# A two-block transformer kernel on one core: who empties PSUM and splits the weights, when the second layer's conditioning is streamed, and how the planner sets priorities

## The chip, the cores and the metric

The kernel runs on one core of a Trainium2 chip. It uses TensorE (PE) for matrix products, VectorE (DVE) and ScalarE (ACT) for all elementwise work, GpSimd (POOL) for a little preparation, and the queue of SyncE (SP) for nearly all DMA. The metric is the device time of one execution in microseconds (us). Before the change it is 1009.37 us, the median of three runs (1007.86 to 1009.71).

## The reference

256 tokens of width 1024 pass through a first block of two layers and a second block of two layers. Cut to what matters here:

```python
cond = silu(c)
for i in range(2):                                   # first block
    sh1, sc1, g1, sh2, sc2, g2 = split(cond @ ada_w[i] + ada_b[i], 6)
    h = rms_norm(x, norm_mix[i]) * (1 + sc1) + sh1
    y = chunked_relpos_attention(h, ...) if i == 0 else chunked_spatial_gating(h, ...)
    x = x + g1 * y
    h = rms_norm(x, norm_ffn[i]) * (1 + sc2) + sh2
    x = x + g2 * (square(relu(h @ ffn_w1[i])) @ ffn_w2[i])
for l in range(2):                                   # second block
    proj = rms_norm(x, pre_norm[l]) @ w_in[l]
    ya = differential_attention(...) * silu(ag)      # 4 heads
    yb = grouped_query_attention(...) * silu(bg)     # 8 heads
    x = x + rms_norm(concat(ya, yb) @ w_out[l], post_norm[l])
```

The attention of the first block has 16 heads of width 64 and a relative-position bias; each token sees its own chunk of 64 and all earlier ones. The gating layer (gMLP) applies gelu to 6144 columns, normalises half of them, mixes positions in windows of 128 and multiplies. All data is fp32.

## The kernel before, in words

**Products.** Tokens lie in two halves of 128, t=0 and t=1. Each fp32 operand is split into a high part (rounded to fp32r) and a low part (the rest), and a product is three fp32r matmuls, high by high, high by low and low by high (`mm3`, L782 to L784). Transposes (`tr`, L810) and the attention's own small matmuls (L770) are fp32.

**Weights.** All weights come as items of 128 x 1024 in the order of `stream_items`, in loads of two items (1 MB, L842) into four `raw` slots. A weight item is split on chip by `item`: a cast to the high part (ACT, L881, or DVE, L882) and a subtraction to the low part (DVE, L885). A slot is free again when its items have been used. Conditioning weights (`ada_w`) run through the same slots, but DVE multiplies them with the condition vector, either as a dot product per 128 rows of a transposed block (`adc`, L748 plus an accumulator read) or as a scaled add into a row (`adg`, L740), after which `fin_gate` spreads the row. (l, m) names the m-th of the six vectors of layer l; `BY_ROWS` lists those that use the second way.

**Stages.** `run` calls attention, FFN0, gMLP, FFN1 and the second block's layers 0 and 1. The attention first projects the eight row blocks k into six PSUM banks (`w("aqk", k)`, `w("avq", k)`), then computes scores, softmax (ACT's Exp, L695, with DVE's L748 for bias and maximum), values and the output projection (weights `ao`). `out_proj` projects t=0 and t=1 into two banks each (c=0, 1). `resid` multiplies by the gate and adds to x (L721), `sumsq` sums squares (L931 on ACT, L933 on DVE), `norm_scale` computes 1/rms with Ln and Exp and scales (L968, L970), and `transpose_split` transposes, applies the conditioning (L1015, L1021) and splits (L988 on ACT, L990 on DVE) into the operands of the next stage.

**Who runs what, and when.** Every operation goes into a planner (`Sched`). An operation may have alternatives on two engines. `round` plays a model timeline: on each engine it takes, among the operations that can start about now, the one with the smallest priority number; the sequence that comes out is each engine's fixed program order. `schedule` repeats this four times: after each round every operation gets a due time, worked backwards from its users, and the next round takes the due times as priorities. The sequence of the best round by the model's clock is kept. ACT's function tables (exp, gelu, silu) are loaded where the order needs another one (L1642).

Of the kernel before, what the change touches and what calls it, by code (L numbers as in the profile page):

```python
# [47 lines left out]
BY_ROWS = ((0, 2), (0, 5), (1, 2), (1, 5), (0, 3))  # L48
# [10 lines left out]
def stream_items():  # L59
    s = []  # L60
    for k in range(KT):
        s += [("adc", 0, 1, k), ("adc", 0, 0, k), ("aqk", k), ("avq", k)]
    for x, y in ((ada_items(0, (2, 4)), [("a2", j, 1, q) for j in (1, 2) for q in range(4)]),
                 (ada_items(0, (3,)), [("ao", k) for k in range(KT)])):
        n = len(y)
        for i, it in enumerate(y):
            s.append(it)
            s += x[len(x) * i // n:len(x) * (i + 1) // n]
    s += pair_stream(NFF, ("w1", 0), ("w2", 0), LAGF, ada_items(0, (5,)) + ada_items(1, (0, 1, 2)))
    e = ada_items(1, (3, 4, 5))  # L70
    for g in range(6):
        for q in range(4):
            s.append(("bv", g, q))
            if len(e) > 12:
                s.append(e.pop(0))
    s += pair_stream(NCB, ("bu",), ("bo",), LAG, e)
    s += pair_stream(NFF, ("w1", 1), ("w2", 1), LAGF)
    for l in range(2):
        s += [("xs", l, BQ, q) for q in range(4)]
        s += [("kv", l, q) for q in range(2)]  # L80
        s += [("ws", l, AQ + 128 * i) for i in range(4)]
        s += [("ws", l, AK + 128 * i) for i in range(4)]
        for c in (AV, AG, BG):
            s += [("xs", l, c, q) for q in range(4)]
        s += [("so", l, k) for k in range(KT)]
    return s
# [244 lines left out]
class Sched:  # L331
# [6 lines left out]
    EXTRA = {"DVE": 0.6}  # L338

# [60 lines left out]
    def schedule(self, spaces, slots, rounds=4):  # L400
# [4 lines left out]
        for i in range(rounds):  # L405
# [6 lines left out]
            if best is None or self.clock < best[0]:  # L412
                best = self.clock, [(o, alt, tab, [b.off for b in o.bufs]) for o, alt, tab in out], \
                    {b: b.off for b in self.fixed}, [(o, o.eng, o.start, o.fin) for o in self.ops]
            due = {}
            for o in sorted(self.ops, key=lambda o: o.start, reverse=True):
                t = o.start if o.eng == "PE" else self.clock
                for u in o.users:
                    if o in u.deps:
                        t = min(t, due[u] - latency(o, u.eng) - (o.fin - o.start))  # L420
                due[o] = t
            for o in self.ops:
                o.pri = due[o] - (self.RUSH if o.crit else 0.0)
        self.clock = best[0]
        for o, o.eng, o.start, o.fin in best[3]:
            pass
        for b in self.fixed:
            b.off = best[2][b]
        return best[1]
# [226 lines left out]
class Prog:  # L656
# [188 lines left out]
    def item(self):  # L845
# [30 lines left out]
        else:  # L876
# [6 lines left out]
            self.prev_split = S.op(alts[:1] if i < POS["w1", 0, 0] else alts, [src], [hi], after=after, pri=pri,  # L883
# [222 lines left out]
    def setup(self):  # L1106
# [15 lines left out]
        self.hooks[1] = [lambda pri: load(self.x[1].v(), io["xin"][:, 1, :], 1.46, pri)]  # L1122
# [12 lines left out]
    def attention(self):  # L1135
# [54 lines left out]
        for j, n in ((0, 0), (1, 0), (2, 0), (0, 1)):  # L1190
            for t in range(2):
                self.copy(qkv[j][n][t].v(), acc[t, j + 3 * n].v(), 512, psum=True)

        def second(j):
# [6 lines left out]
            for t in range(2):  # L1201
                self.copy(qkv[j][1][t].v(), ps[t].v(), 512, psum=True)
# [19 lines left out]
        for i in range(4):  # L1222
            self.act(nb[i].v(), nb[i].v(), D, scale=-1.0, dve=True)
# [4 lines left out]
        for h in range(16):  # L1228
# [4 lines left out]
            if h % 2 == 0:  # L1233
# [4 lines left out]
                self.act(qT.v(), ps.v()[:, 0:256], 256, scale=gqk.v(), psum=True, dve=True)  # L1238
                kk = kd[blk % 2]
                for i in range(2):  # L1240
                    self.copy(kk.v(i)[i * 64:(i + 1) * 64, i * 256:(i + 1) * 256], ps.v()[i * 64:(i + 1) * 64, 256:512], 256,
                              psum=True)
# [16 lines left out]
            self.copy(pT.v(), ps.v()[:, 0:384], 384, psum=True)  # L1259
# [29 lines left out]
    def ffn(self, l):  # L1289
# [5 lines left out]
        gate = self.mod(l, 5) if l == 1 else None  # L1295
# [368 lines left out]
```

## Time and profile before

| | |
|---|---|
| median of three runs | 1009.37 us |
| the profiled execution, its own time | 1009.61 us |
| its span | 1007.8 us |
| PE busy | 976.2 us (97%) |
| DVE busy | 776.7 us (77%) |
| ACT busy | 568.0 us (56%) |
| mean granted TensorE clock | 0.992 |
| chain that ended last | PE 79%, DVE 9%, ACT 5%, DMA 4% |

The span is what the profiler saw from the first to the last instruction; the time of a run includes a little around it. Busy times of engines overlap, so they don't add up. "Idle before" is time in which an engine had nothing it could do, with the instruction that released it. All tiles of a kind lie in one large buffer (`arena` for fp32, `arena_r` for split operands, `raw` for loaded weights, `banks` for PSUM), so the rows tell an operation by its line and shape.

### The profile page before, as it was taken

The page shows a single profiled execution, that of the slowest core. Times are in us where ns is not written, and L with a number is a line of the kernel's source. Part 1 is how long each engine was busy: PE and PEld are TensorE (multiplying, and loading weights), DVE is VectorE, ACT ScalarE, POOL GpSimd, SP SyncE. Part 2 cuts the span into 40 slices and gives each one's busy share as a digit, 9 for nine tenths or more (in the row PEclk, how much of TensorE's full clock was granted, in tenths as well). Part 3 has the DMA queues.
Part 4 walks back from the last instruction along what each step waited for, and adds up shares of the span by engine and source line. Part 5 has one row for each costly group of instructions (what it writes and reads, how often), then busy time and mean ns, then how long its engine had stood idle before and what let it go on. Part 6 is the DMA issues. An engine that isn't in the chain of part 4 may idle for free.

```text
span 1007.8 us, 14849 instructions
## 1 busy us (share of the span) xinstructions
PE 976.2 (97%) x5716; PEld 851.7 (85%) x5716; DVE 776.7 (77%) x1308; ACT 568.0 (56%) x1052; POOL 24.7 (2%) x60
## 2 busy tenths in 40 slices
PE   6999988999999999999999999999999999899997
PEld 5768776899999888899999899999989888799886
DVE  6899989988877986977767855645697786877982
ACT  6578736544445655644455744445455676655781
POOL 1000000010000000000000000030000000000000
PEclk9999998999999999999999999999999999899999
DMA  8987585898775595766463555565545333443401
GB/s 321 359 316 263 210 334 183 359 364 324 290 281 203 207 383 204 292 228 232 170 242 133 177 197 172 207 193 203 179 161 188 113 121 119 160 168 128 166 1 42
DMA packets 32121, 216.50 MB, mean 215 GB/s; under 512 B 3825, under 2 KB 4081, under 8 KB 7217
## 3 DMA queue, kind: packets, MB, share of 16 engines
q1 hardware_dynamic: 30816, 211.98, 56.9%
q0 software_dynamic: 1232, 3.56, 1.4%
q8 instruction: 45, 0.74, 0.3%
q14 instruction: 28, 0.22, 0.1%
HBM read 214.48 MB, written 1.05 MB: 214 GB/s over the span
## 4 chain that ended last, share of the span: by engine, by line
PE 79%; DVE 9%; ACT 5%; DMA 4%; issue 2%; SPq 0%; DVEq 0%; ACTq 0%
PE banks L782 24%; PE banks L783 24%; PE banks L784 24%; PE banks L770 4%; DMA raw<-in_wall 4%; DVE arena_r L885 3%; PE banks L810 3%; DVE arena L721 2%; ACT arena_r L881 1%; ACT arena L695 1%; DVE arena L740 1%; DVE arena L748 1%; DVE arena_r L990 1%; DMA arena<-in_xin 1%; ACT arena L710 1%
## 5 line engine op out<-in xcount | busy, mean ns | idle before, releaser
L782 PE MATMUL banks<-arena_r 128*128 128x256 f32 (+1 forms) x1632 | 563.9, 346 | 7.7 <-ACT arena_r L988 5.2
L783 PE MATMUL banks<-arena_r 128*128 128x256 f32 (+1 forms) x1632 | 554.0, 339 | 1.5 <-DVE arena_r L885 1.4
L784 PE MATMUL banks<-arena_r 128*128 128x256 f32 (+1 forms) x1632 | 553.4, 339 | 1.6 <-DVE arena_r L990 1.6
L885 DVE TENSOR_TENSOR arena_r<-raw,arena_r 128x1024 fp32r<-128x1024 f32 x300 | 359.7, 1221 | 41.8 <-ACT arena_r L881 40.4
L782 PEld LDWEIGHTS banks<-arena_r 128*128 128x128 f32 x1632 | 310.9, 191 | 43.3 <-ACT arena_r L988 8.9
L784 PEld LDWEIGHTS banks<-arena_r 128*128 128x128 f32 x1632 | 310.5, 190 | 38.3 <-DVE arena_r L990 4.7
L783 PEld LDWEIGHTS banks<-arena_r 128*128 128x128 f32 x1632 | 311.2, 191 | 35.3 <-DVE arena_r L885 4.6
L881 ACT CAST arena_r<-raw 128x1024 fp32r<-128x1024 f32 x265 | 270.5, 1044 | 85.9 <-DMA raw<-in_wall 43.4
L695 ACT ACTIVATE arena<-banks 128x256 f32<-128x256 f32 (+1 forms) x104 | 45.0, 434 | 147.2 <-PE banks L784 145.1
L988 ACT ACTIVATE arena_r<-arena 128x256 fp32r<-128x256 f32 (+1 forms) x120 | 55.8, 475 | 78.5 <-DVE arena L740 49.6
L740 DVE SCALAR_TENSOR_TENSOR arena<-banks,arena 128x256 f32<-128x256 f32 (+1 forms) x84 | 38.1, 453 | 60.7 <-ACT arena L695 42.8
L748 DVE CUSTOM_DVE_ANT_0 arena<-raw,arena 128x1024 f32<-128x1024 f32 x56 | 71.7, 1281 | 14.5 <-DMA raw<-in_wall 13.1
L695 ACT ACTIVATE arena<-arena 128x256 f32<-128x256 f32 (+8 forms) x159 | 65.1, 416 | 23.9 <-DVE arena L740 9.1
L990 DVE SCALAR_TENSOR_TENSOR arena_r<-arena,arena_r 128x256 fp32r<-128x256 f32 (+1 forms) x120 | 58.3, 494 | 24.6 <-ACT arena_r L988 23.1
L770 PE MATMUL banks<-arena 128*128 128x64 f32 (+4 forms) x448 | 70.3, 292 | 4.5 <-DMA arena<-in_ident 3.6
L770 PEld LDWEIGHTS banks<-arena 128*128 128x128 f32 x448 | 60.6, 196 | 10.1 <-ACT arena L695 3.6
L810 PE MATMUL banks<-arena 128*128 128x128 f32 x356 | 55.7, 281 | 10.1 <-DVE arena L731 4.3
L710 ACT COPY arena<-banks 128x512 f32<-128x512 f32 (+4 forms) x100 | 47.7, 488 | 31.2 <-PE banks L784 13.7
L810 PEld LDWEIGHTS banks<-arena 128*128 128x128 f32 x356 | 44.0, 147 | 21.5 <-DVE arena L731 4.6
L721 DVE TENSOR_TENSOR arena<-arena 128x512 f32<-128x512 f32 (+6 forms) x128 | 51.4, 433 | 7.6 <-ACT arena L695 3.2
L740 DVE SCALAR_TENSOR_TENSOR arena<-raw,arena 128x1024 f32<-128x1024 f32 x40 | 51.3, 1282 | 3.8 <-DMA raw<-in_wall 3.6
L721 DVE TENSOR_TENSOR arena<-banks,arena 128x512 f32<-128x512 f32 (+1 forms) x48 | 30.0, 641 | 15.3 <-PE banks L784 6.8
(45 smaller groups left out, 330.5 us busy)
## 6 DMA issues: line engine op xcount, KB each, us to landing
raw<-in_wall SPq DMA_DIRECT2D x194, 1024.0 KB, 4.9
raw<-in_wall SPq DMA_DIRECT2D x8, 512.0 KB, 9.1
arena<-in_nbias SPq DMA_DIRECT2D x4, 512.0 KB, 6.5
arena<-in_rows POOLq DMA_DIRECT2D x3, 512.0 KB, 6.0
arena<-in_xin SPq DMA_DIRECT2D x2, 512.0 KB, 5.9
out_dram<-arena SPq DMA_DIRECT2D x4, 256.0 KB, 2.4
arena<-in_dbias POOLq DMA_DIRECT2D x2, 384.0 KB, 3.6
arena<-in_wsT POOLq DMA_DIRECT2D x1, 512.0 KB, 5.9
```

What stands on the lines that cost most here:

```text
L695: nc.scalar.activation(out=res(out), in_=res(in_), func=func, scale=res(scale), **kw, **({"accum_out": res(accum)} if accum is not None el ...
L721: alt = ("DVE", 0.068 + n / 960.0, lambda: nc.vector.tensor_tensor(out=res(out), in0=res(a), in1=res(b), op=op))
L740: return self.S.op(("DVE", dur, lambda: nc.vector.scalar_tensor_tensor(out=res(out), in0=res(a), scalar=res(s), in1=res(b), op0=op0, op1=o ...
L748: return self.S.op(("DVE", dur, lambda: nc.vector.tensor_tensor_reduce(out=res(junk if out is None else out), in0=res(a), in1=res(b), scal ...
L770: o = self.S.op(("PE", max(n, 96) * 0.00167, lambda: nc.tensor.matmul(res(out), lhsT=res(l), rhs=res(r), start=start, stop=stop)), rd, [ou ...
L782: nc.tensor.matmul(o, lhsT=lh, rhs=rh, start=start, stop=False)
L783: nc.tensor.matmul(o, lhsT=lh, rhs=rl, start=False, stop=False)
L784: nc.tensor.matmul(o, lhsT=ll, rhs=rh, start=False, stop=stop)
L810: nc.tensor.transpose(res(o), res(i), res(ident))
L881: alts = [("ACT", 0.093 + D / 1200.0, lambda: nc.scalar.copy(out=res(hi), in_=res(src))), ("DVE", 0.068 + D / 1920.0, lambda: nc.vector.te ...
L885: dve = ("DVE", 0.068 + D / 960.0, lambda: nc.vector.tensor_tensor(out=res(lo), in0=res(src), in1=res(hi.f32()), op=ALU.subtract))
L990: self.S.op(("DVE", 0.068 + n / 960.0, lambda: nc.vector.scalar_tensor_tensor(out=res(lo), in0=res(src), scalar=scale, in1=res(hi.f32()), ...
```

## The change

Six edits:

1. In the attention, the copies and scalings that empty PSUM, and the scaling of the bias, have only ACT as an alternative (`both=False`, no `dve=True`).
2. The high-part cast of a weight has only ACT as an alternative, in the whole kernel.
3. `(0, 3)` leaves `BY_ROWS`, so it becomes eight dot products and needs no `fin_gate` matmuls.
4. Layer 1's conditioning moves back in the stream: (1, 2) from FFN0 to gMLP, (1, 5) from gMLP to FFN1.
5. x's second half is loaded right after the first, no longer behind the first weight loads.
6. Due times are worked backwards from a PE timeline from which the model's gaps are taken out (`packed`), instead of from the model's own start times. The best round's priorities are played once more. `shift` is added, but `SHIFTS` is empty.

```diff
-BY_ROWS = ((0, 2), (0, 5), (1, 2), (1, 5), (0, 3))
+BY_ROWS = ((0, 2), (0, 5), (1, 2), (1, 5))
...
-    s += pair_stream(NFF, ("w1", 0), ("w2", 0), LAGF, ada_items(0, (5,)) + ada_items(1, (0, 1, 2)))
-    e = ada_items(1, (3, 4, 5))
+    s += pair_stream(NFF, ("w1", 0), ("w2", 0), LAGF, ada_items(0, (5,)) + ada_items(1, (0, 1)))
+    e = ada_items(1, (2, 3, 4))
...
-    s += pair_stream(NFF, ("w1", 1), ("w2", 1), LAGF)
+    s += pair_stream(NFF, ("w1", 1), ("w2", 1), LAGF, ada_items(1, (5,)))
...
             if best is None or self.clock < best[0]:
-                best = self.clock, [(o, alt, tab, [b.off for b in o.bufs]) for o, alt, tab in out], \
...
-            due = {}
+                best = self.clock, [o.pri for o in self.ops]
+
+            due, packed, gaps, last = {}, {}, 0.0, 0.0
+            for o in sorted((o for o in self.ops if o.eng == "PE"), key=lambda o: o.start):
+                gaps += max(o.start - last, 0.0)
+                packed[o], last = o.start - gaps, o.fin
             for o in sorted(self.ops, key=lambda o: o.start, reverse=True):
-                t = o.start if o.eng == "PE" else self.clock
+                t = packed[o] if o.eng == "PE" else last - gaps
...
-            self.prev_split = S.op(alts[:1] if i < POS["w1", 0, 0] else alts, [src], [hi], after=after, pri=pri,
+            self.prev_split = S.op(alts[:1], [src], [hi], after=after, pri=pri,
...
-        self.hooks[1] = [lambda pri: load(self.x[1].v(), io["xin"][:, 1, :], 1.46, pri)]
+        load(self.x[1].v(), io["xin"][:, 1, :], 1.46, -2000)
...
-                self.copy(qkv[j][n][t].v(), acc[t, j + 3 * n].v(), 512, psum=True)
+                self.copy(qkv[j][n][t].v(), acc[t, j + 3 * n].v(), 512, psum=True, both=False)
...
-            self.act(nb[i].v(), nb[i].v(), D, scale=-1.0, dve=True)
+            self.act(nb[i].v(), nb[i].v(), D, scale=-1.0)
...
-                self.act(qT.v(), ps.v()[:, 0:256], 256, scale=gqk.v(), psum=True, dve=True)
+                self.act(qT.v(), ps.v()[:, 0:256], 256, scale=gqk.v(), psum=True)
...
-        gate = self.mod(l, 5) if l == 1 else None
```

Since the planner sets the order, most of what the program does differently is not in the diff. Line numbers of the changed kernel are 14 to 16 higher: L770, L782 to L784 and L810 are L786, L798 to L800 and L826; L881, L885 and L721 are L897, L901 and L737.

VectorE at the end of the output projection, before: the last items of (0, 3) and of `ao` (L740, L885), then the residual and sum of squares of t=0 (L721, L933).

```order
L740 SCALAR_TENSOR_TENSOR arena<-raw,arena 128x1024
L885 TENSOR_TENSOR arena_r<-raw,arena_r 128x1024
L740 SCALAR_TENSOR_TENSOR arena<-raw,arena 128x1024
L885 TENSOR_TENSOR arena_r<-raw,arena_r 128x1024
L882 CAST arena_r<-raw 128x1024
L721 TENSOR_TENSOR arena<-banks,arena 128x512 x2
L721 TENSOR_TENSOR arena<-arena 128x512 x2
L933 ISA arena<-arena 128x512
L933 ISA arena 128x1
L731 TENSOR_SCALAR arena<-arena 128x1
L721 TENSOR_TENSOR arena<-banks,arena 128x512 x2
L968 TENSOR_SCALAR arena<-arena 128x512
```

The same place after:

```order
L901 TENSOR_TENSOR arena_r<-raw,arena_r 128x1024
L764 ISA arena<-raw,arena 128x1024
L764 ISA arena 128x1
L1006 SCALAR_TENSOR_TENSOR arena_r<-banks,arena_r 128x512
L901 TENSOR_TENSOR arena_r<-raw,arena_r 128x1024
L756 SCALAR_TENSOR_TENSOR arena<-arena 128x1
L737 TENSOR_TENSOR arena<-banks,arena 128x512
L737 TENSOR_TENSOR arena<-arena 128x512
L949 ISA arena<-arena 128x512
L949 ISA arena 128x1
L737 TENSOR_TENSOR arena<-banks,arena 128x512
L737 TENSOR_TENSOR arena<-arena 128x512
```

The eight scaled adds have become dot products (L764) that stand between the splits; the last of them comes ahead of the last split (L901). No cast stands between that split and the residual, and the residual's steps follow c by c.

TensorE at the handover from `ao` to FFN0, before: the end of the output projection, the gate's matmuls (L770), the transposes of t=0's normalised rows, and the first product of FFN0.

```order
L783 MATMUL banks<-arena_r 128x512
L784 MATMUL banks<-arena_r 128x512
L770 MATMUL banks<-arena 128x1 x8
L810 MATMUL banks<-arena 128x128 x8
L782 MATMUL banks<-arena_r 128x512
```

And after:

```order
L799 MATMUL banks<-arena_r 128x512
L800 MATMUL banks<-arena_r 128x512
L826 MATMUL banks<-arena 128x128 x8
L798 MATMUL banks<-arena_r 128x512
L799 MATMUL banks<-arena_r 128x512
```

The gate's matmuls are gone. What the products are is told by the planner's names for them, which stand in no row. Before, the products of t=0 and t=1 alternate to the end of `ao` (two of t=1 behind t=0's last), and what follows the transposes is FFN0. After, t=0's products come earlier; the six products ahead of these transposes are t=1's for k = 2 to 4, the six behind them are its for k = 5 to 7, and FFN0 begins behind those.

ScalarE in gMLP, where the gelu of the first column blocks, Ln and Exp of the two halves' norms and the next gelu need other tables, before:

```order
L695 ACTIVATE arena<-banks 128x256
L881 CAST arena_r<-raw 128x1024
L1642 ACT_TABLE_LOAD
L695 ACTIVATE arena<-arena 128x1 x2
L881 CAST arena_r<-raw 128x1024 x2
L1642 ACT_TABLE_LOAD
L695 ACTIVATE arena<-banks 128x256 x2
```

And after:

```order
L711 ACTIVATE arena<-banks 128x256
L1657 ACT_TABLE_LOAD
L711 ACTIVATE arena<-arena 128x1 x4
L897 CAST arena_r<-raw 128x1024
L1657 ACT_TABLE_LOAD
L711 ACTIVATE arena<-banks 128x256 x2
```

Before, Ln and Exp of one half (x2) stand between two loads, with two casts behind them, and the other half's stand ahead of the preceding load of gelu; after, both halves' (x4) stand between one pair of loads with one cast.

## Rows read from the trace of the kernel before

**Rows 1.** The page, its first part: busy us, share, instructions.
```profile
PE 976.2 (97%) x5716; PEld 851.7 (85%) x5716; DVE 776.7 (77%) x1308; ACT 568.0 (56%) x1052; POOL 24.7 (2%) x60
```

**Rows 2.** Windows, a steady stage: us, busy of each engine, clock, DMA share, GB/s.
```profile
200.00:400.00 200.00, 200.00 (x1141) 175.84 (x1141) 165.43 (x239) 100.89 (x161) 3.05 (x5) 1.00 0.75 286
```

**Rows 3.** Timeline of PE, 147 to 166: start, us, engine, line, tiles, idle before.
```profile
147.51 1.84 PE L770 MATMUL banks<-arena 128*128 128x1 f32 x16
150.63 1.09 PE L810 MATMUL banks<-arena 128*128 128x128 f32 x8 [1.28 <-ACT arena L970]
153.55 0.79 PE L782 MATMUL banks<-arena_r 128*128 128x512 f32 x1 [1.82 <-ACT arena_r L988]
154.14 0.63 PE L783 MATMUL banks<-arena_r 128*128 128x512 f32 x1
154.57 0.63 PE L784 MATMUL banks<-arena_r 128*128 128x512 f32 x1
...
160.15 0.48 PE L782 MATMUL banks<-arena_r 128*128 128x512 f32 x1
160.47 0.40 PE L783 MATMUL banks<-arena_r 128*128 128x512 f32 x1
160.70 0.39 PE L784 MATMUL banks<-arena_r 128*128 128x512 f32 x1
...
165.75 0.51 PE L784 MATMUL banks<-arena_r 128*128 128x512 f32 x1 [0.59 <-DVE arena_r L990]
```

**Rows 4.** Windows of the attention.
```profile
64.00:100.00 36.00, 34.76 (x193) 27.93 (x193) 35.06 (x87) 31.70 (x82) 2.07 (x4) 1.00 0.69 250
100.00:130.00 30.00, 29.27 (x165) 22.62 (x164) 29.02 (x76) 20.25 (x58) 1.44 (x2) 1.00 0.55 201
...
140.00:147.00 7.00, 5.77 (x24) 4.22 (x24) 6.54 (x8) 2.77 (x3) 0.00 (x0) 1.00 1.01 408
```

**Rows 5.** Timeline of DVE, end of the output projection.
```profile
143.39 1.22 DVE L885 TENSOR_TENSOR arena_r<-raw,arena_r 128x1024 fp32r<-128x1024 f32 x1
...
145.67 1.37 DVE L721 TENSOR_TENSOR arena<-banks,arena 128x512 f32<-128x512 f32 x2 [0.38 <-PE banks L784]
```

**Rows 6.** Groups by line and shape, DVE in 58 to 147: busy, mean ns, idle.
```profile
L713 DVE COPY arena<-banks 128x512 f32<-128x512 f32 x3 | 2.1, 691 | 1.3 <-PE banks L784 1.3
L701 DVE TENSOR_SCALAR arena<-arena 128x1024 f32<-128x1024 f32 x2 | 1.4, 690 | 0.0
...
L701 DVE TENSOR_SCALAR arena<-banks,arena 128x256 f32<-128x256 f32 x3 | 1.3, 476 | 0.0
```

**Rows 7.** Timelines of DVE and ACT, start.
```profile
15.74 1.28 DVE L748 CUSTOM_DVE_ANT_0 arena<-raw,arena 128x1024 f32<-128x1024 f32 x1
...
26.48 1.05 ACT L881 CAST arena_r<-raw 128x1024 fp32r<-128x1024 f32 x1 [5.61 <-DMA raw<-in_wall]
```

**Rows 8.** Timelines of ACT and PE, gMLP.
```profile
414.87 1.28 ACT L1642 ACT_TABLE_LOAD   x1
...
419.10 1.28 ACT L1642 ACT_TABLE_LOAD   x1
...
420.83 0.39 PE L782 MATMUL banks<-arena_r 128*128 128x256 f32 x1 [1.34 <-ACT arena L695]
```

**Rows 9.** Timeline of PE, second block, layer 0 to 1.
```profile
870.60 1.09 PE L810 MATMUL banks<-arena 128*128 128x128 f32 x8 [1.60 <-DVE arena L968]
873.43 0.79 PE L782 MATMUL banks<-arena_r 128*128 128x512 f32 x1 [1.74 <-ACT arena_r L988]
```

**Rows 10.** Casts of DVE and the window, 780 to 975.
```profile
L882 DVE CAST arena_r<-raw 128x1024 fp32r<-128x1024 f32 x13 | 8.8, 685 | 2.1 <-PE banks L784 2.1
...
780.00:975.00 195.00, 191.34 (x1124) 166.39 (x1123) 154.88 (x334) 131.11 (x297) 2.65 (x5) 0.98 0.36 128
```

**Rows 11.** Waits of the load queue (SP), 60 to 147: us, times, longest.
```profile
SPq L842 <- DVE arena L748: 35.0, 7, 11.0
```

**Rows 12.** The page, its fifth part: the casts of ACT.
```profile
L881 ACT CAST arena_r<-raw 128x1024 fp32r<-128x1024 f32 x265 | 270.5, 1044 | 85.9 <-DMA raw<-in_wall 43.4
```

More of the change, by code (lines that the diff above doesn't have):

```diff
@@ L338 @@
     EXTRA = {"DVE": 0.6}
+    SHIFTS = ()
     def __init__(self):
@@ L412, in schedule @@
             if best is None or self.clock < best[0]:
-                best = self.clock, [(o, alt, tab, [b.off for b in o.bufs]) for o, alt, tab in out], \
-                    {b: b.off for b in self.fixed}, [(o, o.eng, o.start, o.fin) for o in self.ops]
-            due = {}
+                best = self.clock, [o.pri for o in self.ops]
[3 more added lines that the diff above has]
+                packed[o], last = o.start - gaps, o.fin
             for o in sorted(self.ops, key=lambda o: o.start, reverse=True):
-                t = o.start if o.eng == "PE" else self.clock
+                t = packed[o] if o.eng == "PE" else last - gaps
                 for u in o.users:
@@ L423, in schedule, with shift @@
                 o.pri = due[o] - (self.RUSH if o.crit else 0.0)
-        self.clock = best[0]
-        for o, o.eng, o.start, o.fin in best[3]:
-            pass
-        for b in self.fixed:
-            b.off = best[2][b]
-        return best[1]
+        pri = list(best[1])
+        for seed in self.SHIFTS:
+            self.shift(best[1], pri, seed)
+        for o, o.pri in zip(self.ops, pri):
+            pass
+        out = self.round(spaces, slots)
+        return [(o, alt, tab, [b.off for b in o.bufs]) for o, alt, tab in out]
+    @staticmethod
+    def shift(base, pri, seed):
+        rng = np.random.default_rng(seed)
+        lo, hi = min(base), max(base)
+        mid, width = rng.uniform(lo, hi), rng.choice([8.0, 20.0, 60.0])
+        size, share = rng.choice([0.7, 2.0, 5.0]), rng.choice([0.1, 0.4, 1.0])
+        for i, b in enumerate(base):
+            if abs(b - mid) < width and rng.random() < share:
+                pri[i] += size * rng.standard_normal()
     def round(self, spaces, slots):
@@ L1201, in second @@
             for t in range(2):
-                self.copy(qkv[j][1][t].v(), ps[t].v(), 512, psum=True)
+                self.copy(qkv[j][1][t].v(), ps[t].v(), 512, psum=True, both=False)
         def norms(n):
@@ L1241, in attention @@
                     self.copy(kk.v(i)[i * 64:(i + 1) * 64, i * 256:(i + 1) * 256], ps.v()[i * 64:(i + 1) * 64, 256:512], 256,
-                              psum=True)
+                              psum=True, both=False)
                 s1, s0 = self.bank(SB), self.bank(SB)
@@ L1258, in attention @@
             pT = self.F(384)
-            self.copy(pT.v(), ps.v()[:, 0:384], 384, psum=True)
+            self.copy(pT.v(), ps.v()[:, 0:384], 384, psum=True, both=False)
             g = h // 4
```

## The prediction

> **What bounds the kernel now.** I read the page's busy times first, then windows along the span, then TensorE's (PE) timeline wherever its busy time falls short, and last the engines that release it there. The reader should see that PE is busy for 976.2 us, 97% of the span [rows 1], and 200.00 of 200 us in a steady stage [rows 2]. There, only less PE work could help, and the change removes nothing but eight small gate matmuls. So all that can be won lies at the stage boundaries. The largest is where the first attention hands over to the first feed-forward layer (FFN0). At 147.51 PE has used up its products and does 128x1 matmuls; then it waits 1.28 us for the norm before the transposes (150.63) and 1.82 us more for ScalarE (ACT) to write the first transposed operand (153.55). After that break its matmuls start 0.43 us apart (154.14, 154.57) at half clock, 1.2 GHz, against 0.23 at 160.47 to 160.70 at full clock; the token half t=1 repeats the chain, up to a last wait at 165.75 [rows 3]. What brings it there is VectorE (DVE): busy 35.06 of 36 and 29.02 of 30 us through the scores [rows 4], it finishes the last output-projection split at 143.39 + 1.22 = 144.6 and starts the residual of t=0 at 145.67, after 0.38 us of waiting for PE [rows 5]. Two products of t=1 (three matmuls of 0.23 us each, 0.68) lie between t=0's last one and 147.51, so that one ended at 146.1.
>
> **Attention and its boundary.** Two things change. (a) DVE loses three 128x512 copies (2.1 us), two 128x1024 scalings (1.4) and three 128x256 scalings (1.3), all ahead of the last split: 4.8 us [rows 6]. ACT gets them at about its own durations; it is busy 31.70 of 36 us in the first part [rows 4], and the 256-wide scalings and one 1024-wide one add 2 to 3 us there, which leaves it at 94 to 96%: hidden, but barely. The eight conditioning items of (0,3) change from scaled adds to dot products, equally long on DVE, and the eight gate matmuls behind them go. (b) At the start x1's load no longer queues behind two weight loads, and the second weight's low-part subtraction no longer waits behind the 1.28 us conditioning dot product at 15.74; ACT's cast that waits 5.61 us for a refilled slot until 26.48 [rows 7] should come some 1.4 us earlier, and with it the first projection, which runs at DVE's pace. So the last split ends at 144.6 - 4.8 - 1.4 = 138.4. Four products of t=0 are left then in the new order (2.7 us), and t=0 ends at 141.1 instead of 146.1.
>
> PE can follow, since the new order holds back twelve products of t=1 (8.2 us): six stand between t=0's end and its transposes, six behind them; before, t=1 alternated with t=0 and two were left. The norm chain took 150.63 - 146.1 = 4.5 us, and about half a microsecond less where c=0's residual runs ahead of c=1's, as it does in the new order: six products (4.1) cover it. From the transposes to the first operand it was 2.9 us, which the other six cover. The second chain (t=1's) finds six products of FFN0 ahead of it; I leave 1 us idle in all. From t=0's end to the point that before reached at 165.75, PE has 12 + 9 products (14.4 us), 20 transposes (8 take 1.09, so 2.7) and that 1 us: 18.1, against 165.75 - 146.1 = 19.6. Without long waits I expect no half-clock stretch. The gain is 5.0 + 1.5 = 6.5 us. If t=0 ends no earlier it is 1.5; if the idle time goes too and the start gives more, 10. I take 6.5, since DVE's busy time, the nearest row, allows it.
>
> One page speaks against giving the evacuations to one engine. What rows 4 show is DVE full and ACT not: 35.06 against 31.70 of 36 us. The Trainium skill, "TensorEngine Tiling (Array Packing)", section "PSUM Bottleneck", advises using both ScalarE and VectorE to empty PSUM; by it (a) would earn nothing, and the sum would stand near the first rival's time, while by the rows the fuller engine is the one that is relieved. That the page holds for a kernel in which both are equally full, no run here shows.
>
> **gMLP.** Before, the two halves' Ln and Exp stand between table loads of 1.28 us each, with two casts between, one load at 414.87 and its partner back to gelu at 419.10 (four around the stage where two are left); PE waits 1.34 us for the gelu at 420.83 [rows 8]. In the new order one pair of loads serves both halves and one cast of 1.05 us leaves the stretch, so the gelu can come 1 to 2 us earlier. I take -1.0, bounds 0 (a late weight holds the remaining cast, as ACT's casts often do [rows 12]) and -1.3.
>
> **Second block, layer 0 to 1.** The same chain leaves PE idle for 1.60 us before its transposes (870.60) and 1.74 before its first product (873.43) [rows 9]. The new order puts eight products of t=1 before the transposes instead of seven, and one behind them instead of none: 2 x 0.68 = -1.4. About 2 us of idle time stay, so I leave the half clock after it as it is. Bounds 0 and -3.8 (with the slow clock gone as well: about twelve matmuls at the 0.2 us that rows 3 show).
>
> **What it adds.** PE's order changes between fp32 and fp32r matmuls 34 times more, 17 round trips. The first interval after a return is 0.32 us (160.15 to 160.47) against 0.23 [rows 3]: 17 x 0.09 = +1.5, bounds 0 (where PE waits anyway) and +3 (if going to fp32 costs as much). The high-part casts that DVE still had go to ACT: 13 of them, 0.69 us each, lie in 780 to 975, where ACT is busy for 131.11 of 195 us [rows 10]; at its 1.04 us that is 13.6 us more, 74%. I cost it at nothing, since a quarter of ACT's time is left there, with up to +3 for casts that stand ahead of a softmax step. The later conditioning of layer 1 moves 10 us of DVE work from FFN0 to FFN1, where PE is the bound and DVE has room (165.43 of 200 in such a stage [rows 2]): 0.
>
> **Sum**, against the profiled execution's own 1009.61 us (span 1007.8 and 1.8 around it; the median of the runs is 1009.37, so it is a typical one): -6.5 - 1.0 - 1.4 + 1.5 = -7.4, so 1002.2.
>
> **Rivals.** First: the last split doesn't come earlier, since the loads bound it. For it: DMA was busy all of 140 to 147 (share 1.01) [rows 4]. Against: the load queue had waited 35.0 us for DVE's dot products to free slots [rows 11], while DMA stood at 0.55 in 100 to 130. Then the boundary gives 1.5, and half the added switches hide: 1009.61 - 1.5 - 1.0 - 1.4 + 0.8 = 1006.5.
> Second: it doesn't do what it says. Only eight large evacuations and scalings move in a whole attention, and priorities made from planned times may order the work about as before; then PE's list is as long as it was and what DVE is spared is idle time: no term counts, 1009.6. Against: the order differs visibly at the places above.
> Third, slower: ACT, in order, becomes late. Each of the 34 casts that move behind the attention (35 in all, one of them at its end) stands before exponentials and evacuations and, waiting for its weights, holds them: 1.04 us and a share of the 43.4 us that 265 casts waited on DMA (0.16 each) [rows 12], 1.2 us a cast. It is decided at eight casts fully on PE's path (8 x 1.2 = 9.6, 1011.8); with ten, 1014. For it: block 2's short matmuls need ACT often; against: ACT is 67% busy there and DVE is spared the casts at the same time.
>
> **How the numbers follow.** Forecast case 0.60 (its own range 997 to 1006), loads 0.16, no effect 0.10, ACT late 0.14. A difference under 0.2% (1007.35 to 1011.4) can't be told from none in this kernel. Faster: nearly all of the first two, 0.75; same 0.11; slower 0.14. The range goes from 995.5 (boundary 10, block 2 at -3.8) to 1011, which leaves the last rival and a little below outside.
>
> **What would show it.** Right: t=0's residual near 140, PE busy from there to 160 with no gap over 1 us and the granted clock at full around 153; no gap at the gMLP's gelu; gaps at 870 shorter by 1.4 in sum. Wrong: ACT casts waiting on DMA up to 145 with the add still there (first rival); PE waits on ACT between 780 and 975 above those before (third); or half clock again behind the handover, which alone costs 2 us. The forecast fails altogether if gaps of a few tenths, spread over the steady stages, appear in a PE timeline that had none.

## The result, and the profile after

The changed kernel takes 996.1 us (median of four runs, 995.85 to 996.75) against 1009.54 for the kernel before in the same session; the ratio is 0.9864, 95% interval 0.9838 to 0.9889. That is 13.4 us, where 7.4 were forecast: faster, inside the range, and by nearly twice the forecast. The profiled execution took 996.07 us, its span is 994.0. First the page of the changed kernel, its busy times [rows 1] and its chain of waits:

```profile
PE 970.2 (98%) x5700; PEld 849.9 (86%) x5700; DVE 751.0 (76%) x1269; ACT 599.3 (60%) x1094; POOL 23.3 (2%) x58
...
PE 90%; ACT 5%; DVE 3%; issue 1%; DMA 1%; SPq 0%; DVEq 0%; ACTq 0%
```

PE is busy for 6.0 us less, 1.84 of them the gate's matmuls. The granted clock doesn't show less half clock as the reason for the rest: its mean in the profiled execution is 0.990, where it was 0.992. The idle times ahead of its matmuls sum to 17.6 us instead of 25.0. DVE gave up 26 us, ACT took 31. The chain that ended last is now PE for 90%. Next the handover from `ao` to FFN0 on PE, the place of [rows 3]:

```profile
145.68 1.04 PE L826 MATMUL banks<-arena 128*128 128x128 f32 x8
146.47 0.48 PE L798 MATMUL banks<-arena_r 128*128 128x512 f32 x1
...
155.10 0.66 PE L826 MATMUL banks<-arena 128*128 128x128 f32 x4
...
156.98 0.60 PE L826 MATMUL banks<-arena 128*128 128x128 f32 x4
```

The transposes of t=0 come six products of t=1 behind t=0's last one and don't wait, nor do the first product of FFN0, six products later, and the first transposes of t=1 (155.10, 156.98): no row names a releaser. DVE at the same place [rows 5]:

```profile
136.70 1.22 DVE L901 TENSOR_TENSOR arena_r<-raw,arena_r 128x1024 fp32r<-128x1024 f32 x1
...
139.75 0.69 DVE L737 TENSOR_TENSOR arena<-banks,arena 128x512 f32<-128x512 f32 x1 [1.77 <-PE banks L800]
...
141.82 0.69 DVE L737 TENSOR_TENSOR arena<-banks,arena 128x512 f32<-128x512 f32 x1
```

The last split ends at 136.70 + 1.22 = 137.9 (138.4 was forecast); the residual of t=0's first half starts at 139.75, the second's at 141.82, after t=0's last product at 141.6 (146.1 before, 141.1 forecast). That end is no longer set by the split: PE runs without a wait of more than 0.15 us from 118.52 to 157.83. The clock, in windows of 50 us (the column before the DMA share):

```profile
100.00:150.00 50.00, 45.52 (x231) 36.07 (x231) 46.64 (x110) 34.68 (x81) 0.13 (x1) 0.93 0.74 287
150.00:200.00 50.00, 49.75 (x303) 43.65 (x302) 45.71 (x56) 32.49 (x57) 0.00 (x0) 1.00 0.72 265
850.00:900.00 50.00, 47.81 (x318) 42.93 (x317) 42.30 (x78) 34.58 (x66) 0.00 (x0) 1.00 0.47 175
```

Behind the handover (150 to 200) and in the second block (850 to 900) it is at full speed throughout; before, the same two windows show 0.93. It is at half now at two other places: at the start and in the attention, where PE waits 3.1 us for a copy of ACT. PE's timeline at the start:

```profile
11.76 3.68 PE L826 MATMUL banks<-arena 128*128 128x128 f32 x16 [4.70 <-ACT arena L986]
16.39 0.80 PE L798 MATMUL banks<-arena_r 128*128 128x512 f32 x1 [0.95 <-ACT arena_r L1004]
16.98 0.63 PE L799 MATMUL banks<-arena_r 128*128 128x512 f32 x1
```

And in the attention:

```profile
118.52 0.90 PE L826 MATMUL banks<-arena 128*128 128x128 f32 x3 [3.10 <-ACT arena L726]
...
121.51 0.78 PE L798 MATMUL banks<-arena_r 128*128 128x512 f32 x1
122.08 0.63 PE L799 MATMUL banks<-arena_r 128*128 128x512 f32 x1
```

In both, intervals of 0.43 or more between matmuls (16.98 to 17.41, 122.08 to 122.51) follow a long wait. So the attention lost and the handover gained. PE's busy time is the first number behind the length of the window, before:

```profile
60.00:130.00 70.00, 68.03 (x374) 53.87 (x373) 67.45 (x164) 55.91 (x146) 3.51 (x6) 1.00 0.65 239
130.00:200.00 70.00, 63.27 (x343) 52.78 (x342) 65.99 (x87) 38.89 (x67) 1.44 (x2) 0.95 0.78 301
```

And after:

```profile
60.00:130.00 70.00, 63.85 (x329) 49.13 (x328) 67.51 (x167) 59.84 (x152) 2.32 (x5) 0.95 0.70 271
130.00:200.00 70.00, 69.75 (x411) 60.78 (x410) 63.15 (x86) 44.21 (x75) 0.00 (x0) 1.00 0.72 272
```

The gMLP's table loads on ACT [rows 8]:

```profile
405.71 1.28 ACT L1657 ACT_TABLE_LOAD   x1
407.00 0.95 ACT L711 ACTIVATE arena<-arena 128x1 f32<-128x1 f32 x4
407.86 1.04 ACT L897 CAST arena_r<-raw 128x1024 fp32r<-128x1024 f32 x1
408.91 1.28 ACT L1657 ACT_TABLE_LOAD   x1
```

The loads start 3.2 us apart (4.2 before, with two more loads ahead of them), Ln and Exp of both halves stand between them, and PE has no wait there. Second block, layer 0 to 1, PE [rows 9]:

```profile
857.25 1.04 PE L826 MATMUL banks<-arena 128*128 128x128 f32 x8
...
859.58 0.50 PE L798 MATMUL banks<-arena_r 128*128 128x512 f32 x1 [0.60 <-ACT arena_r L1004]
...
864.69 0.50 PE L799 MATMUL banks<-arena_r 128*128 128x512 f32 x1 [1.59 <-DVE arena L747]
```

The waits of 1.60 and 1.74 us ahead of t=0's transposes and first product have become none and 0.60; one of 1.59 us has come up 5 us later, so 2.19 us are left of 3.34, and the matmuls behind them come at full clock.

To see where the time went I counted the columns of all fp32r matmuls along each PE timeline (1,900,544 in either kernel) and read the times at equal counts. The column is the changed kernel's time minus that of the kernel before, at the end of each stretch of the latter:

| stretch (times of before) | forecast for it | lead at its end | gained in it |
|---|---|---|---|
| start, attention, handover to FFN0 (to 209) | -6.5, switches apart | -7.4 | -7.4 |
| FFN0 (to 400) | 0 | -7.9 | -0.5 |
| gMLP's table loads (to 439) | -1.0 | -9.5 | -1.6 |
| gMLP to FFN1 (to 712) | 0 | -10.1 | -0.6 |
| end of FFN1, second block's start (to 827) | 0 | -11.4 | -1.3 |
| second block, layer 0 to 1 (to 884) | -1.4 | -14.1 | -2.7 |
| to the end | 0 | -13.8 | +0.3 |

These come from one profile each, and two executions of the same order differ too: cast_free, interleaved, swap_back and cast_three (below) run the changed kernel's order on PE, DVE and ACT for the first 58 us, and at the columns that before reaches at 53 us the five lead by 0.8, 0.8, 1.3, 1.7 and 2.2 us. Differences of about 1 us between two rows or two runs are not shown by this count.

### The profile page after: what moved, and what is told of

Its sections match the earlier page's. It is cut to its first block, busy times and chain, and to the rows that moved or that the text cites. A ratio compares the mean times of both kernels' runs of the same rounds, so it can differ in the third digit from the quotient of the medians.

```text
span 994.0 us, 14855 instructions
## 1 busy us (share of the span) xinstructions
PE 970.2 (98%) x5700; PEld 849.9 (86%) x5700; DVE 751.0 (76%) x1269; ACT 599.3 (60%) x1094; POOL 23.3 (2%) x58
## 4 chain that ended last, share of the span: by engine, by line
PE 90%; ACT 5%; DVE 3%; issue 1%; DMA 1%; SPq 0%; DVEq 0%; ACTq 0%
PE banks L798 28%; PE banks L800 27%; PE banks L799 27%; PE banks L786 4%; PE banks L826 3%; ACT arena L711 2%; DVE arena L737 1%; ACT arena_r L897 1%; ACT arena L726 1%; DVE arena_r L901 1%; DVE arena L764 1%; DMA arena<-in_xin 1%; ACT arena L1037 0%; DVE arena L756 0%; DVE arena_r L1006 0%
## 5 line engine op out<-in xcount | busy, mean ns | idle before, releaser
L798 PE MATMUL banks<-arena_r 128*128 128x256 f32 (+1 forms) x1632 | 563.4, 345 | 1.9 <-ACT arena_r L1004 1.5
L800 PE MATMUL banks<-arena_r 128*128 128x256 f32 (+1 forms) x1632 | 552.7, 339 | 0.0
L901 DVE TENSOR_TENSOR arena_r<-raw,arena_r 128x1024 fp32r<-128x1024 f32 x300 | 360.1, 1221 | 60.4 <-ACT arena_r L897 59.2
L800 PEld LDWEIGHTS banks<-arena_r 128*128 128x128 f32 x1632 | 310.1, 190 | 35.7 <-DVE arena_r L1006 1.8
L798 PEld LDWEIGHTS banks<-arena_r 128*128 128x128 f32 x1632 | 310.5, 190 | 34.1 <-ACT arena_r L1004 2.4
L897 ACT CAST arena_r<-raw 128x1024 fp32r<-128x1024 f32 x300 | 305.1, 1044 | 48.3 <-PE banks L800 24.7
L764 DVE CUSTOM_DVE_ANT_0 arena<-raw,arena 128x1024 f32<-128x1024 f32 x64 | 82.0, 1281 | 11.7 <-DMA raw<-in_wall 11.1
L711 ACT ACTIVATE arena<-arena 128x256 f32<-128x256 f32 (+9 forms) x161 | 67.4, 425 | 33.1 <-DVE arena L949 13.1
L786 PE MATMUL banks<-arena 128*128 128x64 f32 (+3 forms) x432 | 68.4, 294 | 3.5 <-DMA arena<-in_ident 3.3
L786 PEld LDWEIGHTS banks<-arena 128*128 128x128 f32 x432 | 59.9, 196 | 12.9 <-issue 3.5
L826 PE MATMUL banks<-arena 128*128 128x128 f32 x356 | 57.0, 287 | 9.9 <-ACT arena L986 4.7
L826 PEld LDWEIGHTS banks<-arena 128*128 128x128 f32 x356 | 45.2, 150 | 20.3 <-ACT arena L986 6.5
L726 ACT COPY arena<-banks 128x512 f32<-128x512 f32 (+3 forms) x102 | 48.6, 492 | 22.1 <-PE banks L826 10.9
L737 DVE TENSOR_TENSOR arena<-arena 128x512 f32<-128x512 f32 (+6 forms) x128 | 52.0, 433 | 8.6 <-DMA arena<-in_rows 3.2
L756 DVE SCALAR_TENSOR_TENSOR arena<-raw,arena 128x1024 f32<-128x1024 f32 x32 | 41.0, 1280 | 3.4 <-DMA raw<-in_wall 3.2
L737 DVE TENSOR_TENSOR arena<-banks,arena 128x512 f32<-128x512 f32 (+1 forms) x48 | 30.2, 642 | 14.9 <-PE banks L800 6.9
```

The costliest lines, as they stand in the source:

```text
L711: nc.scalar.activation(out=res(out), in_=res(in_), func=func, scale=res(scale), **kw, **({"accum_out": res(accum)} if accum is not None el ...
L737: alt = ("DVE", 0.068 + n / 960.0, lambda: nc.vector.tensor_tensor(out=res(out), in0=res(a), in1=res(b), op=op))
L756: return self.S.op(("DVE", dur, lambda: nc.vector.scalar_tensor_tensor(out=res(out), in0=res(a), scalar=res(s), in1=res(b), op0=op0, op1=o ...
L764: return self.S.op(("DVE", dur, lambda: nc.vector.tensor_tensor_reduce(out=res(junk if out is None else out), in0=res(a), in1=res(b), scal ...
L786: o = self.S.op(("PE", max(n, 96) * 0.00167, lambda: nc.tensor.matmul(res(out), lhsT=res(l), rhs=res(r), start=start, stop=stop)), rd, [ou ...
L798: nc.tensor.matmul(o, lhsT=lh, rhs=rh, start=start, stop=False)
```

## The experiments

Theory A was that the new priorities make the gain; theory B that the work taken off DVE in the attention makes it, partly as time and partly through the order that the planner then finds. The medians of the kernel before lie between 1009.5 and 1010.1 in these sessions, so the ratios are what compares. The last two columns are the lead over the kernel before at equal columns, after the handover and at the end of the profiled execution, counted as above. That execution was 3.4 us slower than the median in old_rule (1003.43), 2.5 slower in late_and_stream (999.34) and 3.4 faster in evac_alone (1001.77), so their leads don't go with their medians.

| run | median us | ratio to before, 95% interval | lead at 209 | at the end |
|---|---|---|---|---|
| changed kernel | 996.1 | 0.9864 (0.9838 to 0.9889) | -7.4 | -13.8 |
| old_rule | 1000.04 | 0.9915 (0.9890 to 0.9940) | -3.1 | -6.9 |
| rule_alone | 1007.95 | 0.9983 (0.9968 to 0.9998) | +3.7 | -0.7 |
| evac_both | 1004.11 | 0.9948 (0.9927 to 0.9969) | +0.6 | -4.8 |
| old_stream | 994.13 | 0.9846 (0.9821 to 0.9872) | -9.0 | -14.8 |
| evac_alone | 1005.12 | 0.9940 (0.9916 to 0.9963) | -5.2 | -7.8 |
| interleaved | 1002.73 | 0.9923 (0.9905 to 0.9941) | +0.1 | -6.3 |
| swap_back | 998.07 | 0.9879 (0.9860 to 0.9899) | -5.1 | -11.5 |
| cast_three | 999.36 | 0.9887 (0.9865 to 0.9908) | -4.6 | -10.9 |
| cast_free | 999.75 | 0.9900 (0.9880 to 0.9920) | -6.8 | -10.1 |
| x1_late | 995.14 | 0.9858 (0.9836 to 0.9881) | -9.7 | -14.8 |
| rows_and_cast | 1000.76 | 0.9909 (0.9888 to 0.9931) | -5.0 | -8.0 |
| late_and_stream | 996.81 | 0.9861 (0.9840 to 0.9882) | -5.6 | -10.2 |

**old_rule** and **rule_alone**: the planner's rule taken out of the changed kernel, and put alone into the kernel before.

```diff
-            for o in sorted((o for o in self.ops if o.eng == "PE"), key=lambda o: o.start):
-                gaps += max(o.start - last, 0.0)
-                packed[o], last = o.start - gaps, o.fin
...
-                t = packed[o] if o.eng == "PE" else last - gaps
+                t = o.start if o.eng == "PE" else self.clock
```

> The changed kernel with the planner's old rule for due times (and without the last replay), all other edits kept. Theory A (the new priorities make the gain): the handover falls back towards the old form, 1003 to 1008. Theory B (what was taken off VectorE in the attention and the stream make it, the planner then holds back t=1 by itself): the planned order still holds back nine or ten products of t=1 behind t=0's end, so 997 to 1000, with the gMLP and second-block gaps partly back.

> The kernel before with the new rule for due times alone. Theory A: most of the gain, 998 to 1002. Theory B: t=1 still alternates with t=0 in the output projection and two products are left, so the handover stays and the time is 1005 to 1010.

Both fit theory B better than A. Without the rule 0.9915 is left, so the rule carries some 4 to 5 of the 13.4 us; alone it carries 1.7. With the rule alone the planned order has three products of t=1 left behind t=0, and PE waits as before (its timeline, to the transposes and the first product):

```profile
153.48 1.10 PE L826 MATMUL banks<-arena 128*128 128x128 f32 x8 [0.95 <-ACT arena L986]
156.69 0.50 PE L798 MATMUL banks<-arena_r 128*128 128x512 f32 x1 [2.12 <-ACT arena_r L1004]
```

It is 3.7 us late there and gains 4.4 later. With the old rule and all else changed, the planner holds back twelve, as with the new one; but in that profile PE still waits at the handover (1.44 us at 156.31, 1.41 at 161.67, 0.60 at 163.37), so holding them back is not all that the rule does there.

**evac_both** and **evac_alone**: the attention's PSUM copies and scalings free to go to DVE again; and, in the kernel before, taken from it as the only edit.

```diff
-                self.copy(qkv[j][n][t].v(), acc[t, j + 3 * n].v(), 512, psum=True, both=False)
+                self.copy(qkv[j][n][t].v(), acc[t, j + 3 * n].v(), 512, psum=True)
...
-            self.act(nb[i].v(), nb[i].v(), D, scale=-1.0)
+            self.act(nb[i].v(), nb[i].v(), D, scale=-1.0, dve=True)
```

> The changed kernel with the attention's copies and scalings free to go to VectorE again. Theory B: VectorE is full again, t=0 ends 2 to 4 us later, 998 to 1001. Theory A and the theory that the stream does it: 996 to 997.

> The kernel before with one edit: the attention's copies and scalings go to ScalarE alone. If the relief of VectorE is the main term: the planner, by its old rule, already holds back ten products of t=1 behind t=0's last one, and the handover gains 5 to 7 us: 1001 to 1004. If it works only together with the new rule and the stream: 1006 to 1009.

evac_both lost more than either theory said: 8 us of the 13.4. Nine products of t=1 are held back in its planned order, but the splits come too late for that: in this window DVE is busy for 9.96 of 10 us and PE for 6.13:

```profile
130.00:140.00 10.00, 6.13 (x17) 3.65 (x16) 9.96 (x20) 3.14 (x3) 0.00 (x0) 0.85 0.91 352
```

The last split of `ao` ends at 142.21 + 1.22 = 143.4, against 137.9. Two splits of FFN0's weights stand behind it, after a cast of ACT, and end at 144.97 + 2.36 = 147.3, ahead of t=0's residual:

```profile
142.21 1.22 DVE L901 TENSOR_TENSOR arena_r<-raw,arena_r 128x1024 fp32r<-128x1024 f32 x1
...
144.97 2.36 DVE L901 TENSOR_TENSOR arena_r<-raw,arena_r 128x1024 fp32r<-128x1024 f32 x2 [1.40 <-ACT arena_r L897]
```

evac_alone, with the old rule and the old stream, is 5.2 us ahead after the handover in its profile, as theory B has it. In time its ratio of 0.9940 is 6.0 us; its median of 1005.12 lies a little above the 1001 to 1004 that was expected, beside a kernel before at 1010.03. Nine products of t=1 are held back, where before it were two, and its last split on DVE ends at 136.21 + 1.22 = 137.4:

```profile
136.21 1.22 DVE L885 TENSOR_TENSOR arena_r<-raw,arena_r 128x1024 fp32r<-128x1024 f32 x1
```

It still has the gate's matmuls behind `ao`, and one PE wait of 2.90 us:

```profile
146.07 1.84 PE L770 MATMUL banks<-arena 128*128 128x1 f32 x16
150.81 0.80 PE L782 MATMUL banks<-arena_r 128*128 128x512 f32 x1 [2.90 <-ACT arena_r L988]
```

**swap_back** and **interleaved** keep the changed kernel's finished order and alter one thing in it, so that the planner can't answer. swap_back issues on DVE, at the same places, the nine evacuations and scalings that DVE had before. interleaved moves the twelve products of t=1 up, each pair behind t=0's.

```diff
-                    alt[2]()
+                    self.swap.get(o, alt[2])()      # nine ops: the same work as a DVE instruction
```

```diff
+            for g in range(2, KT):
+                if e[0] is self.ao[0, 1, g]:            # t=0, c=1, row block g
+                    new += [late[0, g], late[1, g]]     # t=1's pair right behind it
```

> The changed kernel's finished order, with nine evacuations and scalings of the attention (the nine that VectorE had before) issued on VectorE at the same places. If VectorE's time itself is what counts: its splits come up to 5 us later, 999 to 1001. If it counts only through the order that the planner then makes: 996 to 997, or a little less, since ScalarE is relieved where TensorE waits 3.1 us for it at 118.5.

> The changed kernel's finished order, with only the twelve products of t=1 (k = 2 to 7 of the output projection) moved up on TensorE, each pair directly behind t=0's for the same k. If the hold-back hides the norm chain: t=0 ends 5 to 8 us later, nothing covers its chain, 4 to 6 us idle or at half clock, 1000 to 1003. If the earlier end of the splits did it: 996 to 998.

interleaved is 7.4 us behind the changed kernel at the handover, the whole lead, and on PE the chain shows again, with half clock behind it:

```profile
152.79 1.63 PE L827 MATMUL banks<-arena 128*128 128x128 f32 x8 [2.27 <-ACT arena L987]
155.82 0.80 PE L799 MATMUL banks<-arena_r 128*128 128x512 f32 x1 [1.41 <-ACT arena_r L1005]
156.41 0.63 PE L800 MATMUL banks<-arena_r 128*128 128x512 f32 x1
```

swap_back's last split ends at 139.40 + 1.22 = 140.6, 2.7 us later than the changed kernel's, where up to 5 was expected, and PE is 2.2 us later after the handover:

```profile
139.40 1.22 DVE L911 TENSOR_TENSOR arena_r<-raw,arena_r 128x1024 fp32r<-128x1024 f32 x1
...
141.98 0.69 DVE L747 TENSOR_TENSOR arena<-banks,arena 128x512 f32<-128x512 f32 x1 [1.30 <-PE banks L810]
```

So of what evac_both loses at the handover (8.0), 2 to 3 is the time of these nine operations on DVE (3 if counted from 53 us on, since swap_back leads there by 0.8 more). The rest is not pure order: the planner put fourteen such operations on DVE there (7.5 us), not nine (5.3), and the two causes are not separated. In time, swap_back's interval overlaps that of the changed kernel.

**cast_three**: in the finished order, the casts of the first three `ao` items on DVE, to take them out of ACT's way before 118.52.

```diff
+            if it in (("ao", 0), ("ao", 1), ("ao", 2)):
+                self.swap[self.prev_split] = alts[1][2]    # the cast as a DVE copy
```

> The changed kernel's finished order, with the high-part casts of the first three output-projection items on VectorE, at the same places. TensorE's wait of 3.10 us at 118.52 is for a copy that stands behind exponentials and these three casts (3.1 us) on ScalarE. If the casts are what makes ScalarE late there: the wait falls to about 1 us and the half clock after it goes, 993 to 995. If VectorE (2.1 us more) is as late then: 996 to 997.

At 999.36 it came out above both answers (its interval overlaps the changed kernel's), though the 3.10 us wait fell to 0.88. DVE, 2.1 us fuller, became late twice (1.85 at 113.63, 1.37 at 129.11), and each time the clock fell (column before the DMA share). From 60 to 209 the waits sum to 6.1 us, as in the changed kernel, but more time passes at half clock: 0.71 and 0.66 in the windows below, where the changed kernel has 0.84 and 1.00. PE's timeline:

```profile
113.63 0.50 PE L800 MATMUL banks<-arena_r 128*128 128x512 f32 x1 [1.85 <-DVE arena_r L904]
...
116.55 0.90 PE L827 MATMUL banks<-arena 128*128 128x128 f32 x3 [0.88 <-ACT arena L727]
...
129.11 0.88 PE L827 MATMUL banks<-arena 128*128 128x128 f32 x4 [1.37 <-DVE arena L738]
```

The windows around the two waits:

```profile
110.00:120.00 10.00, 7.27 (x25) 4.73 (x24) 9.80 (x24) 7.23 (x26) 0.00 (x0) 0.71 0.48 166
...
130.00:140.00 10.00, 10.00 (x45) 8.79 (x45) 8.45 (x13) 4.37 (x7) 0.00 (x0) 0.66 0.97 394
```

**cast_free**: the casts behind the attention free to go to DVE.

```diff
-            self.prev_split = S.op(alts[:1], [src], [hi], after=after, pri=pri,
+            self.prev_split = S.op(alts[:1] if i < POS["w1", 0, 0] else alts, [src], [hi], after=after, pri=pri,
```

> The changed kernel with the high-part casts behind the attention free to go to VectorE again (36 do). The handover's order is the same. If the casts cost ScalarE nothing, as the prediction has it: 995 to 998. If ScalarE was late because of them in the second block: 991 to 994, with the last layer's loss of about 2 us gone. If VectorE is the one that needs the room: 998 to 1001.

999.75: the third answer, 3.7 us slower than the changed kernel by the medians (the intervals just touch). The handover is equal to 0.5 us; of the lead, 1.2 go between 400 and 572 and 1.6 at the second block's handover, where PE now waits once for 1.92 us and loses clock (its timeline):

```profile
863.51 0.50 PE L798 MATMUL banks<-arena_r 128*128 128x512 f32 x1 [1.92 <-ACT arena_r L1004]
```

The window around it:

```profile
850.00:870.00 20.00, 18.06 (x74) 13.79 (x72) 15.79 (x27) 12.99 (x31) 0.00 (x0) 0.91 0.36 143
```

In the changed kernel this handover lies in 850 to 900, where the clock is 1.00 (above).

**x1_late**, **old_stream**, **rows_and_cast**, **late_and_stream**: the early load of x, the stream and `BY_ROWS` taken back, alone and in pairs.

```diff
-        load(self.x[1].v(), io["xin"][:, 1, :], 1.46, -2000)                            # x1_late
+        self.hooks[1] = [lambda pri: load(self.x[1].v(), io["xin"][:, 1, :], 1.46, pri)]
...
-    e = ada_items(1, (2, 3, 4))                                                         # old_stream, with BY_ROWS
+    e = ada_items(1, (3, 4, 5))
```

> The changed kernel with x's second half loaded behind two weight loads again. By the prediction the early load starts the projection 1.4 us earlier: 997 to 998. If the half clock that the new start has from 16.4 to 20.8 ate that gain, or the projection waits for VectorE anyway: 995 to 997.

> The changed kernel with the conditioning streamed as before ((0,3) as scaled adds with its gate matmuls, (1,2) in FFN0, (1,5) in gMLP). If the stream carries part of the handover: seven products of t=1 are left behind t=0 and the gate's matmuls are back in the chain, 998 to 1002. If it only spreads VectorE work to where there is room: 996 to 997.

> The changed kernel with (0, 3) as scaled adds again and the casts behind the attention free. Eleven products of t=1 stay behind t=0 in the planned order. If the scaled adds alone make the old stream's better handover: 992 to 995. If that came from where layer 1's conditioning runs: 996 to 998.

> The changed kernel without two of its edits: x's second half loaded behind two weight loads, and layer 1's conditioning streamed as early as before; (0, 3) stays a dot product. The planned handover is that of the run with x's late load, which had no 3 us wait in the attention. If the two edits are neutral by themselves and only shift where the planner puts things: 993 to 996, so no slower than the changed kernel. If either gave something: 997 to 999.

Neither the early load nor the stream gave anything that can be measured: x1_late and old_stream are nominally 1 and 2 us faster than the changed kernel, with overlapping intervals, old_stream against its expectation; neither has the 3.1 us wait in the attention. old_stream holds back only seven products of t=1, and PE waits 1.35 and 1.02 us at its handover (150.90, 155.61), yet it leads by 9.0 there: in that order, more than seven held-back products were not needed. In x1_late the last split on DVE ends at 134.40 + 1.22 = 135.6 (the changed kernel: 137.9):

```profile
134.40 1.22 DVE L901 TENSOR_TENSOR arena_r<-raw,arena_r 128x1024 fp32r<-128x1024 f32 x1
```

Together (late_and_stream) they did not add up: 996.81, between its two answers. rows_and_cast, at 1000.76, was outside both answers; it has cast_free's edit in it and is as slow, but what the scaled adds do alone was not run. old_stream, at 0.9846, is the fastest kernel run; that it beats the changed kernel is not shown.

## Why the prediction was right, and where a size was wrong

The main step came out in its numbers: the last split at 137.9 (138.4), t=0's end at 141.6 (141.1), the norm chain covered by the twelve products, no half clock behind it, -7.4 at the handover with its share of the switches (-6.5 without). evac_alone and evac_both show that it rests on DVE's relief, interleaved that in this order it is collected by the held-back products. The prediction had told the order and its cause apart only in part: it took the twelve products as given, while the planner makes them out of the relief.

Part of that agreement is luck, in two places. First, the split's 138.4 was DVE's spared 4.8 us and an earlier start of 1.4. The runs don't show these two terms: the same nine operations put back in the finished order move the split by 2.7 (swap_back), the relief as the only edit brings it 7.2 earlier (evac_alone, 144.6 to 137.4), and with x loaded late it comes 2.3 earlier than with x loaded early (x1_late). Nor was DVE's own time what it ended on. Before, DVE had waited for a load ahead of its last two items of (0, 3), and ACT ahead of its cast of the last item of `ao` (their timelines):

```profile
139.69 1.29 DVE L740 SCALAR_TENSOR_TENSOR arena<-raw,arena 128x1024 f32<-128x1024 f32 x1 [2.21 <-DMA raw<-in_wall]
...
142.11 1.05 ACT L881 CAST arena_r<-raw 128x1024 fp32r<-128x1024 f32 x1 [1.45 <-DMA raw<-in_wall]
```

In the changed kernel the loads themselves come earlier; DMA's share was 0.55 and 1.01 in the same two windows before:

```profile
100.00:130.00 30.00, 25.52 (x124) 18.94 (x124) 29.20 (x80) 22.96 (x62) 0.13 (x1) 0.89 0.74 287
...
140.00:147.00 7.00, 7.00 (x36) 5.91 (x35) 6.81 (x13) 2.84 (x6) 0.00 (x0) 1.00 0.40 157
```

So the first rival (loads bound the last split) had its condition right and fell by its consequence: the loads did not stay where they were. That a less busy DVE frees the slots earlier fits the load queue's waits for DVE [rows 11]; no run tests it by itself. Second, the attention lost what the forecast put at nothing ("hidden, but barely"): from 60 to 130 PE is busy for 63.85 us instead of 68.03, most of it the 3.10 us wait for ACT at 118.52, and the handover gained more than 6.5 to make up for it. x1_late and old_stream, without that wait, lead by 9.7 and 9.0.

The second rival (no effect) fell. So did the third (ACT late behind the attention): between 780 and 975 PE is busy for 192.77 of 195 us, 191.34 before. The place where ACT is late, behind exponentials and casts at 118.52, lies ahead of the casts that moved.

The start's 1.4 us is not shown. At the count of columns that before reaches at 53 us the five profiles of the new order lead by 0.8 to 2.2, x1_late, with the late load, by 1.5, and evac_alone, whose order up to there is that of the kernel before, by 1.1. In the changed kernel's profile the first ten fp32r matmuls run at half clock; in two of the five (swap_back, cast_three) they don't.

The switches were about right: returns from fp32 to fp32r in the PE timeline went from 105 to 121, 16 more where 17 were planned, and most of the first intervals behind them are 0.31 to 0.32 us again. At 0.09 each that is 1.4 us (1.5 forecast); no run isolates it.

What was mis-sized are three terms. The block-2 term: -1.4 was forecast, with the half clock left as it was; -2.7 was measured, with 1.15 us less waiting and a clock that stays up, which the prediction had only as its bound. How much the clock carries is not separated: x1_late, with half clock there, still gains 2.4 in that stretch. The gMLP term: -1.0 against -1.6, more than the wait of 1.34 alone. And the casts, costed at nothing: cast_free prices them at about 3 us of gain, spread over the boundaries behind the attention, where DVE no longer has a cast ahead of the subtraction or residual that PE waits for. That mechanism is argued from the places of the loss; that the sum is 3 us and not 1 is not settled, as the two kernels were not timed side by side. The 1.3 us gained between 712 and 827 have no cause that was tested.

"TensorEngine Tiling (Array Packing)", section "PSUM Bottleneck", of the Trainium skill advises both engines for emptying PSUM; here the measurement decides against it: free to use both, the kernel was at 0.9948 instead of 0.9864. The Trainium skill's "Perfetto Trace Analysis", section "Optimizing Scalar/DVE Operations", fits: where DVE is saturated, offloading to Scalar may make sense; DVE was busy 35.06 of 36 us and ACT 31.70.

## What to carry to other kernels

Where PE is the bound, look for the stage boundaries and ask what independent products can stand between the last product of one half and its norm; twelve of them (8.2 us) were worth 7 us here, seven did as well in old_stream, and the relief of the engine that delivers the last operand let the planner make them. When a planner makes the order, test an edit twice, with the planner free and with the finished order kept: the first gave 8 us for the evacuations, the second 2 to 3, and the planner had moved fourteen in the one and nine in the other. Don't judge an edit by the sum of PE's waits alone: cast_three waits as long as the changed kernel in the attention, with more half clock, and gains 4.1 us less between 53 and 209. And before reading 1 us off two profiles, look at how far two executions of the same order lie apart.

## What the runs showed of the hardware

The length of a wait alone doesn't tell whether half clock follows. In the changed kernel waits of 0.60 us at 859.58 and 1.59 at 864.69 left the clock at full; in x1_late the same wait of 1.59 us, without the one of 0.60, was followed by half clock:

```profile
862.09 0.50 PE L799 MATMUL banks<-arena_r 128*128 128x512 f32 x1 [1.59 <-DVE arena L747]
```

The window around it:

```profile
860.00:870.00 10.00, 8.39 (x39) 6.65 (x38) 8.06 (x13) 6.54 (x14) 0.00 (x0) 0.83 0.30 107
```

Nor does the order of instructions. cast_three starts with the changed kernel's order on every engine, waits a little longer ahead of its transposes (4.89 us against 4.70), and its first products come at full clock:

```profile
11.85 3.59 PE L827 MATMUL banks<-arena 128*128 128x128 f32 x16 [4.89 <-ACT arena L989]
```

The window of the first products, in the changed kernel and in cast_three:

```profile
16.00:21.00 5.00, 4.61 (x11) 3.60 (x12) 4.96 (x9) 3.13 (x6) 0.00 (x0) 0.50 1.03 427
16.00:21.00 5.00, 4.53 (x19) 3.47 (x20) 4.96 (x9) 3.02 (x6) 0.00 (x0) 1.00 1.04 428
```

So one profile's half clock at such a place is not a property of the kernel alone. What else decides it, no run here separates.
